# Streaming-encoder layer on one core: second-norm sums from fused additions and squares on ScalarE, stores on three queues, two pairs of the first norm on VectorE, y transposes one tick later

## The chip, the cores and the metric

One core of one Trainium2 chip runs the kernel. The metric is the device time of one execution in microseconds (us); shown is the median of several runs, and beside it one execution that the hardware profiler took.

The engines named below are TensorE (PE in the rows; PEld is its weight load), VectorE (DVE), ScalarE (ACT), GpSimd (POOL) and SyncE (SP). Each works through its instructions in order. Transfers are issued by SP, by POOL or by ACT, each into a queue of its own; only POOL's can add into their destination.

## The reference

The computation is one layer of a hybrid encoder on 1024 tokens of width 1024, all in float32:

```python
mix = hybrid_mixer(x, w_in, b_gate, w_conv, hn_g, w_pool, pool_scale, w_out)
x = layer_norm(ALPHA * x + mix, ln1_g, ln1_b)                            # first norm
x = layer_norm(ALPHA * x + squared_relu_mlp(x, w_ff1, w_ff2), ln2_g, ln2_b)   # second norm

def layer_norm(x, g, b):
    mu = x.mean(-1, keepdims=True)
    var = square(x - mu).mean(-1, keepdims=True)
    return (x - mu) * rsqrt(var + 1e-5) * g + b
```

The mixer projects x to q, k, v, gates and pooling columns, runs a chunkwise mLSTM of four heads (its result per 128 tokens, normalised and gated, is called y below) and a multiscale pooling, and multiplies both by `w_out`. The MLP is `square(relu(x @ w1)) @ w2` with a hidden width of 4096.

## The kernel before, in words

**Number format.** Every f32 matmul is made of three: each operand is split into a high part (a cast on ScalarE, L76) and a low part (a subtraction on VectorE, L77), and `mm3` (L102) issues high x high, high x low and low x high (L103 to L105) into the same PSUM bank.

**Tiles of tokens.** Tokens stand in eight tiles of 128, c = 0 to 7, called tokens 0 to 7 here, in two halves hf = 0 and 1. `z[c, e]` is the accumulator of tile c, column half e (512 wide); `zt[c]` is both halves.

**Order of the work.** The functions at the end of the kernel are called in the order of its text: projections of the first half, of the second half with the mLSTM of the first beside them, and `out_proj(0)` and `out_proj(1)`, the output projection for the two column halves. Side work is put between the matmuls by a clock: `later(lag, fn)` (L111) queues a function, `tick()` (L114) advances the clock by one and runs what is due. A step of a projection (one pair of tiles, 48 matmuls of 512 columns) has two ticks, one in its middle and one at its end. `mlstm(hf)` (L558) splits each tile's mixer into four stages and queues them at four lags; the fourth (after the last `yield` of `mlstm_stages`) transposes y on TensorE (L553) and splits the result into `yTm[c]`, which `out_proj` reads in the second half of the step of the pair that has tile c. Within this, the framework's scheduler settles each engine's final instruction order when the kernel is built, and adds all waits.

**First norm.** `out_proj(e)` goes over pairs cp = 0, 2, 4, 6. For each tile it adds the residual into z (L629) and takes statistics (`bn_stats`, L630). In the pass e = 1 it then aggregates (L633), calls `ln_rsqrt` (L569: a Sqrt on ScalarE, L573, and small VectorE instructions, L574 to L581, with one Newton step) and `ln_apply` (L584) per tile: a ScalarE pass with scale and shift (L588), a multiply by the gain on VectorE (L593 here, L590 for the second norm), and a transfer on POOL that adds the broadcast bias into z (L594). After the pairs cp = 2 and cp = 6 a half is whole, and its z is transposed to the MLP's input (`x1_transpose`, L651, copied to SBUF by ScalarE, L652): half 0 by tasks at lags 3 and 4, half 1 in the job loop at the second job.

**MLP.** Four rounds of two products, each product cut Strassen-fashion into seven jobs of 48 matmuls (i = 1 to 7, `ORDER`, L731). `weights` (L716) loads a 512 KB weight tile by SP (L722) and builds sums of weight blocks by accumulating transfers on POOL (L725); a tile that has been cast for one job grows by another accumulate for the next. In round 0 `x_right` (L754) forms sums of x blocks on VectorE (L746 to L752) and stores them to DRAM by POOL (L762) for the later rounds, where SP loads them (L766). The tiles of the MLP lie in the pool `fq` (21 tiles), which takes the memory of the earlier pool `bigp` (42 tiles), where the gains of the first norm (`gs1`, loaded by POOL at L902) also were.

**Second norm.** `evict2` (L836) adds a product into z (L847). In the last round, jobs 2, 3, 7, 4 are the final ones: statistics are taken of each z (L851). After job 3 the tiles 0 to 3 are aggregated (L857), share one `ln_rsqrt` and go through `ln_apply` and `store` (L866, SP). In job 4, `finish(c)` (L868) does tiles 4 to 7 singly: 4 and 5 by `ln_apply` and `store`; 6 and 7 by (z - mean) x gain (L877) while the root is taken, then x root + bias (L880) and two stores by SP (L881). The gain and bias tiles are `gb2`.

Of the kernel before, what the change touches and what calls it, by code (L numbers as in the profile page):

```python
# [13 lines left out]
ALU = mybir.AluOpType  # L14

P = 128
# [6 lines left out]
def trunk_layer(ctx: ExitStack, tc: tile.TileContext, x, w_in, b_gate, w_conv, hn_g,  # L23
# [534 lines left out]
    def mlstm(hf):  # L558
        for i in range(TT):
            st = mlstm_stages(hf * TT + i)  # L560
            for lag in (max(2 * i - 2, 0), 2 * i + (i == 0), 2 * i + 2, 2 * i + 4):
                later(lag, lambda st=st: next(st, None))
# [6 lines left out]
    def ln_rsqrt(mv, n):  # L569

        v = mv[:, :, 1]
# [28 lines left out]
    def out_proj(e, gs):  # L600
# [3 lines left out]
        for cp in range(0, S // P, 2):  # L604
# [26 lines left out]
            if e == 1:  # L631
                for i in range(2):
                    dve.bn_aggr(mv[:, i, :], st[:, i])  # L633
                r = ln_rsqrt(mv, 2)
                for i in range(2):
                    ln_apply(zt[cp + i], mv, i, r[:, i:i + 1], gs, ln1_b)
# [199 lines left out]
    def evict2(i, ps, r):  # L836
# [4 lines left out]
        for j in range(4):  # L841
            c = t * 4 + j
            zs = z[c, d]
            if r == 0 and i in (1, 6, 5, 4):
# [3 lines left out]
            if final:  # L848
                if c not in ln2:
                    ln2[c] = sml([P, 2, 6], "l2_st", 8)  # L850
                dve.bn_stats(ln2[c][:, d, :], zs)  # L851
            if final and i == 4:
                finish(c)
        if final and i == 3:
            mv = sml([P, 4, 2], "l2_mv4")
            for c in range(4):
                dve.bn_aggr(mv[:, c, :], ln2[c])  # L857
            rr = ln_rsqrt(mv, 4)
            for c in range(4):
                ln_apply(zt[c], mv, c, rr[:, c:c + 1], gb2[:1], ln2_b)  # L860
                store(c)
# [3 lines left out]
    def store(c):  # L865
        sp.dma_start(out[c * P:(c + 1) * P, :], zt[c].rearrange("p e c -> p (e c)"))  # L866

    def finish(c):  # L868
        mv = sml([P, 1, 2], "l2_mv")
        dve.bn_aggr(mv[:, 0, :], ln2[c])  # L870
        if c < 6:
            r = ln_rsqrt(mv, 1)
            ln_apply(zt[c], mv, 0, r, gb2[:1], ln2_b)
            store(c)
            return
        g, b = gb2
        dve.scalar_tensor_tensor(zt[c], zt[c], mv[:, 0, 0:1], g, op0=ALU.subtract, op1=ALU.mult)  # L877
        r = ln_rsqrt(mv, 1)
        for e in C2:
            dve.scalar_tensor_tensor(z[c, e], z[c, e], r, b[:, e, :], op0=ALU.mult, op1=ALU.add)  # L880
            sp.dma_start(out[c * P:(c + 1) * P, e * 512:(e + 1) * 512], z[c, e])  # L881
# [18 lines left out]
    gs1 = [big([P, 512], name="lng") for _ in range(2)]  # L900
    for e in range(2):
# [55 lines left out]
```

## Time and profile before

| | |
|---|---|
| median of 3 runs | 1062.92 us (1061.78 to 1063.1) |
| profiled execution | 1064.35 us |
| its span | 1062.6 us |
| PE busy | 1011.6 us, 95% of the span, 4697 instructions |
| DVE busy | 737.2 us, 69% |
| ACT busy | 446.9 us, 42% |
| POOL busy | 155.6 us, 15% |
| mean granted TensorE clock | 0.983 |
| moved by DMA | 143.29 MB, mean 135 GB/s |

The profiled execution's time holds the span (first to last instruction or transfer of the program, 1062.6 us) and 1.75 us around it. Busy shares are averages over the whole span; the granted clock is a share of TensorE's full speed. Times in rows are microseconds from the span's start unless marked ns.

### The profile page before, as it was taken

The numbers are of one execution on the slowest core, as the hardware profiler recorded it, in microseconds if no ns is written. First come the engines' busy times: TensorE is split into PE (matmuls) and PEld (weight loads), VectorE is DVE, ScalarE is ACT, GpSimd is POOL, SyncE is SP. The second block draws the span as 40 slices with busy tenths as digits, with TensorE's granted clock in tenths as the row PEclk, the third lists the DMA queues.
The fourth block names the chain that finished last, engine by engine and source line by source line (L and its number), as shares of the span: only waits on it lengthen the run. The fifth ranks groups of instructions, "written<-read, shape, count | busy, mean of one in ns | idle before, by whom it ended". The sixth has DMA issues, their size and how long they took to land.

```text
span 1062.6 us, 12549 instructions
## 1 busy us (share of the span) xinstructions
PE 1011.6 (95%) x4697; PEld 826.9 (78%) x4697; DVE 737.2 (69%) x1187; ACT 446.9 (42%) x630; POOL 155.6 (15%) x195
## 2 busy tenths in 40 slices
PE   7999999999989987979999999999999999999991
PEld 5898789778878876858888888888888888888881
DVE  4464775886988445648966478866488875588885
ACT  5334655638322235334433534334524434434441
POOL 2320002312310023200302001302002102001210
PEclk9999999999999998989999999999999999999996
DMA  8411512414421268967807647908737718702728
GB/s 302 135 61 42 158 52 63 137 59 120 159 80 40 60 162 205 272 192 237 154 5 145 196 155 218 159 1 175 223 127 208 138 15 176 257 29 40 143 49 245
DMA packets 64062, 143.29 MB, mean 135 GB/s; under 512 B 4652, under 2 KB 4736, under 8 KB 64000
## 3 DMA queue, kind: packets, MB, share of 16 engines
q1 hardware_dynamic: 41760, 92.09, 26.1%
q0 software_dynamic: 22144, 50.36, 24.8%
q8 instruction: 37, 0.61, 0.2%
q14 instruction: 25, 0.20, 0.1%
q10 hardware_dynamic: 96, 0.03, 0.0%
HBM read 130.90 MB, written 11.57 MB: 134 GB/s over the span
## 4 chain that ended last, share of the span: by engine, by line
PE 82%; DVE 8%; DMA 4%; issue 2%; ACT 1%; POOL 0%; DVEq 0%; SPq 0%; ACTq 0%; POOLq 0%
PE mm L105 17%; PE mm L104 17%; PE mm L103 17%; PE ml L103 5%; PE ml L104 5%; PE ml L105 5%; PE tr L103 5%; PE tr L104 4%; PE tr L105 4%; DMA z<-in_ln_b_dram 2%; DMA w<-in_w_ff_dram 1%; DMA xraw<-in_x_dram 1%; DVE wlo L77 1%; PE tr L651 1%; PE tr L177 1%
## 5 line engine op out<-in xcount | busy, mean ns | idle before, releaser
L77 DVE TENSOR_TENSOR ol<-w,oh 128x1024 fp32r<-128x1024 f32 x112 | 135.6, 1221 | 95.0 <-ACT oh L76 95.0
L103 PE MATMUL mm<-oh,oh 128*128 128x512 f32 x448 | 177.6, 397 | 5.6 <-ACT oh L76 5.6
L76 ACT CAST oh<-w 128x1024 fp32r<-128x1024 f32 x112 | 116.6, 1047 | 152.1 <-PE mm L104 62.6
L104 PE MATMUL mm<-ol,oh 128*128 128x512 f32 x448 | 177.4, 396 | 0.5 <-DVE ol L77 0.5
L105 PE MATMUL mm<-oh,ol 128*128 128x512 f32 x448 | 177.3, 396 | 0.0
L725 POOL DMA_DIRECT2D w<-in_w_ff_dram x64 | 76.9, 1276 | 499.2 <-DVE ol L77 487.4
L103 PEld LDWEIGHTS mm<-oh,oh 128*128 128x128 f32 x448 | 84.8, 189 | 26.0 <-ACT oh L76 6.1
L104 PEld LDWEIGHTS mm<-ol,oh 128*128 128x128 f32 x448 | 84.7, 189 | 20.7 <-DVE ol L77 1.0
L105 PEld LDWEIGHTS mm<-oh,ol 128*128 128x128 f32 x448 | 84.7, 189 | 20.0
L103 PE MATMUL ml<-oh,oh 128*128 128x512 f32 x224 | 88.9, 398 | 0.0
L104 PE MATMUL ml<-ol,oh 128*128 128x512 f32 x224 | 88.8, 396 | 0.0
L105 PE MATMUL ml<-oh,ol 128*128 128x512 f32 x224 | 88.7, 396 | 0.0
L104 PE MATMUL tr<-ol,oh 128*128 128x512 f32 x224 | 88.3, 394 | 0.1
L103 PE MATMUL tr<-oh,oh 128*128 128x512 f32 x224 | 88.3, 394 | 0.0
L105 PE MATMUL tr<-oh,ol 128*128 128x512 f32 x224 | 88.2, 394 | 0.0
L77 DVE TENSOR_TENSOR ol<-xs,oh 128x1024 fp32r<-128x1024 f32 x42 | 51.4, 1224 | 50.7 <-ACT oh L76 50.7
L76 ACT CAST oh<-h 128x1024 fp32r<-128x1024 f32 x40 | 41.7, 1048 | 80.2 <-PE ml L104 24.8
L76 ACT CAST oh<-xs 128x1024 fp32r<-128x1024 f32 x42 | 44.1, 1050 | 66.2 <-PE ml L104 37.3
L77 DVE TENSOR_TENSOR wlo<-raw,whi 128x1024 fp32r<-128x1024 f32 (+1 forms) x44 | 55.2, 1254 | 11.7 <-ACT whi L76 9.0
L76 ACT CAST whi<-raw 128x1024 fp32r<-128x1024 f32 (+1 forms) x44 | 46.0, 1053 | 32.6 <-PE mm L104 13.4
L103 PE MATMUL mm<-xT,whi 128*128 128x512 f32 x144 | 57.3, 398 | 0.1
L104 PE MATMUL mm<-xT,whi 128*128 128x512 f32 x144 | 57.0, 396 | 0.0
(259 smaller groups left out, 1993.0 us busy)
## 6 DMA issues: line engine op xcount, KB each, us to landing
w<-in_w_ff_dram POOLq DMA_DIRECT2D x64, 512.0 KB, 7.5
w<-in_w_ff_dram SPq DMA_DIRECT2D x58, 512.0 KB, 8.2
xs<-xs SPq DMA_DIRECT2D x42, 512.0 KB, 4.7
raw<-in_w_in_dram SPq DMA_DIRECT2D x28, 512.0 KB, 4.3
z<-in_ln_b_dram POOLq DMA_DIRECT2D x14, 512.0 KB, 7.7
xs<-x POOLq DMA_DIRECT2D x12, 512.0 KB, 10.1
raw<-in_w_in_dram SPq DMA_DIRECT2D x8, 520.0 KB, 5.2
raw<-in_w_out_dram SPq DMA_DIRECT2D x8, 512.0 KB, 3.3
```

The source lines that it names most:

```text
L76: act.copy(hi, src)
L77: dve.tensor_tensor(lo, src, hi.bitcast(F32), ALU.subtract)
L103: pe.matmul(ps, lhsT=lh, rhs=rh, start=start, stop=False, skip_group_check=grow)
L104: pe.matmul(ps, lhsT=lh, rhs=rl, start=False, stop=False, skip_group_check=grow)
L105: return pe.matmul(ps, lhsT=ll, rhs=rh, start=False, stop=stop, skip_group_check=grow)
L177: pe.transpose(ps[:, a, b, :], raw[:, b, kc * P:(kc + 1) * P], ident)
L651: pe.transpose(ps[:, j, :], z[hf * TT + j, kb // 4][:, (kb % 4) * P:(kb % 4 + 1) * P], ident)
L725: pool.dma_start(t, w_source(r, ph, q, p), accum_op=ALU.add)
```

## The change

Four places are edited. (1) The fourth lag of `mlstm` goes from 2i + 4 to 2i + 5, capped at 10: for i = 0, 1, 2 of either half the transposes of y come one tick later. (2) In `out_proj(1)`, the pairs cp = 2 and 6 (`late`) no longer use `ln_apply`: VectorE computes (z - mean) x gain in four instructions of 512 columns ahead of `ln_rsqrt`, and z x root + bias in four behind it. For this the bias is loaded as two more tiles (`gs1` has four). (3) In the last round, the final additions into z are one VectorE instruction each that also gives the sum over its 512 columns (`accum_out`); `bn_stats` and `bn_aggr` are gone. `finish(c)` is called for all eight tiles, singly, tiles 0 to 3 behind job 3's evictions: it forms minus the mean, has ScalarE square (z - mean) with the sum as a second output, and takes the root of that. `store` is gone. (4) Stores: tile 5 by POOL, tile 7 by ACT, the others by SP.

```diff
--- before.py
+++ after.py
@@ -558,7 +558,7 @@
     def mlstm(hf):
         for i in range(TT):
             st = mlstm_stages(hf * TT + i)
-            for lag in (max(2 * i - 2, 0), 2 * i + (i == 0), 2 * i + 2, 2 * i + 4):
+            for lag in (max(2 * i - 2, 0), 2 * i + (i == 0), 2 * i + 2, min(2 * i + 5, 10)):
                 later(lag, lambda st=st: next(st, None))
 
 
@@ -566,9 +566,8 @@
     def ln_stats(t, n, tag):
         return sml([P, n, 2, 6], f"{tag}_st{n}"), sml([P, n, 2], f"{tag}_mv{n}")
 
-    def ln_rsqrt(mv, n):
-
-        v = mv[:, :, 1]
+    def ln_rsqrt(v, n):
+
         s, w, t = (sml([P, n], f"l{n}_{i}") for i in "swt")
         act.activation(s, v, AF.Sqrt, bias=epsc)
         dve.tensor_scalar(w, v, EPS, -0.5, op0=ALU.add, op1=ALU.mult)
@@ -631,9 +630,19 @@
             if e == 1:
                 for i in range(2):
                     dve.bn_aggr(mv[:, i, :], st[:, i])
-                r = ln_rsqrt(mv, 2)
+                late = cp % TT == 2
+                if late:
+                    for i, d in ((0, 0), (0, 1), (1, 0), (1, 1)):
+                        zs = z[cp + i, d]
+                        dve.scalar_tensor_tensor(zs, zs, mv[:, i, 0:1], gs[d], op0=ALU.subtract, op1=ALU.mult)
+                r = ln_rsqrt(mv[:, :, 1], 2)
                 for i in range(2):
-                    ln_apply(zt[cp + i], mv, i, r[:, i:i + 1], gs, ln1_b)
+                    if late:
+                        for d in range(2):
+                            zs = z[cp + i, d]
+                            dve.scalar_tensor_tensor(zs, zs, r[:, i:i + 1], gs[2 + d], op0=ALU.mult, op1=ALU.add)
+                    else:
+                        ln_apply(zt[cp + i], mv, i, r[:, i:i + 1], gs[:2], ln1_b)
             if e == 1 and cp % TT == 2:
                 x1_later(cp // TT)
             tick()
@@ -841,44 +850,44 @@
         for j in range(4):
             c = t * 4 + j
             zs = z[c, d]
-            if r == 0 and i in (1, 6, 5, 4):
+            if final:
+                if c not in ln2:
+                    ln2[c] = sml([P, 8], "l2_sum", 8)
+                dve.scalar_tensor_tensor(zs, ps[j], float(sign), zs, op0=ALU.mult, op1=ALU.add,
+                                         accum_out=ln2[c][:, d:d + 1])
+                if i in (3, 4):
+                    finish(c)
+            elif r == 0 and i in (1, 6, 5, 4):
                 dve.scalar_tensor_tensor(zs, zs, ALPHA, ps[j], op0=ALU.mult, op1=op)
             else:
                 dve.tensor_tensor(zs, zs, ps[j], op)
-            if final:
-                if c not in ln2:
-                    ln2[c] = sml([P, 2, 6], "l2_st", 8)
-                dve.bn_stats(ln2[c][:, d, :], zs)
-            if final and i == 4:
-                finish(c)
-        if final and i == 3:
-            mv = sml([P, 4, 2], "l2_mv4")
-            for c in range(4):
-                dve.bn_aggr(mv[:, c, :], ln2[c])
-            rr = ln_rsqrt(mv, 4)
-            for c in range(4):
-                ln_apply(zt[c], mv, c, rr[:, c:c + 1], gb2[:1], ln2_b)
-                store(c)
 
     ln2, gb2 = {}, []
 
-    def store(c):
-        sp.dma_start(out[c * P:(c + 1) * P, :], zt[c].rearrange("p e c -> p (e c)"))
-
     def finish(c):
-        mv = sml([P, 1, 2], "l2_mv")
-        dve.bn_aggr(mv[:, 0, :], ln2[c])
+
+        q = ln2[c]
+        neg, ss, s, w, u, shift = (q[:, k:k + 1] for k in range(2, 8))
+        zf, (g, b) = zt[c], gb2
+        dve.tensor_scalar(neg, q[:, 0:1], q[:, 1:2], -1.0 / 1024, op0=ALU.add, op1=ALU.mult)
+        act.activation(quad("sq"), zf, AF.Square, bias=neg, accum_out=ss)
+        if c >= 6:
+            dve.scalar_tensor_tensor(zf, zf, neg, g, op0=ALU.add, op1=ALU.mult)
+        act.activation(s, ss, AF.Sqrt, bias=epsc, scale=1.0 / 1024)
+        dve.tensor_scalar(w, ss, -0.5 / 1024, -0.5 * EPS, op0=ALU.mult, op1=ALU.add)
+        dve.reciprocal(s, s)
+        dve.scalar_tensor_tensor(u, s, s, w, op0=ALU.mult, op1=ALU.mult)
+        dve.scalar_tensor_tensor(s, u, 1.5, s, op0=ALU.add, op1=ALU.mult)
         if c < 6:
-            r = ln_rsqrt(mv, 1)
-            ln_apply(zt[c], mv, 0, r, gb2[:1], ln2_b)
-            store(c)
+            dve.tensor_tensor(shift, neg, s, ALU.mult)
+            act.activation(zf, zf, AF.Identity, scale=s, bias=shift)
+            dve.tensor_tensor(zf, zf, g, ALU.mult)
+            pool.dma_start(zf, b, accum_op=ALU.add)
+            (pool if c == 5 else sp).dma_start(out[c * P:(c + 1) * P, :], zf.rearrange("p e c -> p (e c)"))
             return
-        g, b = gb2
-        dve.scalar_tensor_tensor(zt[c], zt[c], mv[:, 0, 0:1], g, op0=ALU.subtract, op1=ALU.mult)
-        r = ln_rsqrt(mv, 1)
         for e in C2:
-            dve.scalar_tensor_tensor(z[c, e], z[c, e], r, b[:, e, :], op0=ALU.mult, op1=ALU.add)
-            sp.dma_start(out[c * P:(c + 1) * P, e * 512:(e + 1) * 512], z[c, e])
+            dve.scalar_tensor_tensor(z[c, e], z[c, e], s, b[:, e, :], op0=ALU.mult, op1=ALU.add)
+            (act if c == 7 else sp).dma_start(out[c * P:(c + 1) * P, e * 512:(e + 1) * 512], z[c, e])
 
     proj_o(0)
     small_parameters()
@@ -897,9 +906,10 @@
     proj_qk(1, 0)
     later(1, lambda: mlstm(1))
     proj_p(1)
-    gs1 = [big([P, 512], name="lng") for _ in range(2)]
-    for e in range(2):
-        after(pool.dma_start(gs1[e], ln1_g[0:1, e * 512:(e + 1) * 512].to_broadcast([P, 512])), anchor[0])
+    gs1 = [big([P, 512], name="lngb") for _ in range(4)]
+    for e in range(4):
+        src = (ln1_g, ln1_b)[e // 2][0:1, e % 2 * 512:(e % 2 + 1) * 512]
+        after(pool.dma_start(gs1[e], src.to_broadcast([P, 512])), anchor[0])
     out_proj(0, gs1)
     out_proj(1, gs1)
```

## Rows read from the trace of the kernel before

**Rows 1.** TensorE's waits, whole span: line <- waited for: us in total, times, longest
```profile
PE tr L651 <- DMA z<-in_ln_b_dram: 8.8, 4, 4.0
PE mm L103 <- ACT oh L76: 5.6, 1, 5.6
PE tr L553 <- DVE y L549: 4.9, 3, 2.8
```
**Rows 2.** Timeline of TensorE, L651: start, us, engine, operation [idle before <- releaser]
```profile
380.08 0.74 PE L651 MATMUL tr<-ident,z 128*128 128x128 f32 x5 [2.52 <-DMA z<-in_ln_b_dram]
...
411.92 0.45 PE L651 MATMUL tr<-ident,z 128*128 128x128 f32 x1 [4.01 <-DMA z<-in_ln_b_dram]
414.38 1.30 PE L651 MATMUL tr<-ident,z 128*128 128x128 f32 x5 [2.01 <-DMA z<-in_ln_b_dram]
```
**Rows 3.** Stretches: us, then each engine's busy us, PEclk, DMA share, GB/s
```profile
375.00:385.00 10.00, 7.18 (x32) 5.71 (x31) 5.00 (x14) 3.27 (x6) 1.12 (x2) 0.83 0.56 134
408.00:424.00 16.00, 10.07 (x50) 8.45 (x51) 8.96 (x9) 9.42 (x15) 5.72 (x6) 0.79 1.01 203
424.00:440.00 16.00, 16.00 (x70) 13.01 (x70) 14.94 (x15) 5.40 (x6) 5.54 (x9) 1.00 1.02 341
```
**Rows 4.** Chain of waits, around the transposes of z: start, us, engine and line
```profile
373.43 6.52 DMA z<-in_ln_b_dram
...
404.45 9.79 DMA z<-in_ln_b_dram
...
415.68 0.85 PE ml L103 x2
...
418.80 0.87 PE tr L651 x8
419.67 0.23 PE ml L105
```
**Rows 5.** Timeline of all engines, the tail from 1040 us
```profile
1040.84 0.39 PE L105 MATMUL ml<-oh,ol 128*128 128x512 f32 x1
...
1044.21 0.69 DVE L851 BATCH_NORM_STATS2 l_st<-z 128x6 f32<-128x512 f32 x1
...
1046.56 0.86 POOL L594 DMA_DIRECT2D z<-in_ln_b_dram  x1 [1.78 <-issue]
...
1049.36 1.41 DVE L880 SCALAR_TENSOR_TENSOR z<-z,l_s,lngb 128x512 f32<-128x512 f32 x2
...
1055.84 0.33 SPq L866 DMA_DIRECT2D out_dram<-z  x1
1056.59 0.87 SPq L881 DMA_DIRECT2D out_dram<-z  x2
```
**Rows 6.** Timeline of VectorE, first norm of cp = 6 and job 1's operands
```profile
398.75 0.17 DVE L574 TENSOR_SCALAR l_w<-l_mv 128x2 f32<-128x2 f32 x1
399.08 0.17 DVE L575 RECIPROCAL l_s<-l_s 128x2 f32<-128x2 f32 x1 [0.16 <-ACT l_s L573]
...
401.40 2.50 DVE L593 TENSOR_TENSOR z<-z,lng 128x512 f32<-128x512 f32 x4 [1.30 <-ACT z L588]
...
408.63 1.23 DVE L77 TENSOR_TENSOR ol<-x,oh 128x1024 fp32r<-128x1024 f32 x1 [0.21 <-ACT oh L76]
```
**Rows 7.** Timeline of POOL, mixer's work for token 6 and later stores of x sums
```profile
298.68 1.19 POOL L507 TENSOR_TENSOR vs<-v,g_ep 128x516 f32<-128x516 f32 x1 [6.22 <-DVE ps L352]
...
450.07 0.57 POOL L762 DMA_DIRECT2D xs<-x  x1 [9.63 <-DVE x L752]
```
**Rows 8.** Waits of SP's queue, 395 to 430 us
```profile
SPq L722 <- DVE z L593: 14.1, 1, 14.1
```
**Rows 9.** Groups of ScalarE, whole span: busy us, mean ns, idle before
```profile
L588 ACT ACTIVATE z<-z,l_sh,l_s 128x1024 f32<-128x1024 f32 x14 | 16.6, 1235 | 9.2 <-DVE l_sh L587 9.2
...
L573 ACT ACTIVATE l_s<-l_mv,epsc 128x2 f32<-128x2 f32 (+2 forms) x9 | 2.7, 295 | 37.3 <-DVE l_mv L633 27.6 <-DVE l_mv L870 7.6 <-DVE l_mv L857 2.0
...
L573 ACT ACT_TABLE_LOAD x1 | 1.3, 1283 | 0.0
```

## Prediction, made before the changed kernel was run

> **What bounds the kernel now.** I read the table of TensorE's waits first, because TensorE is busy 95% of the span and a wait counts only where it stands still. There are few such places [rows 1]: the transposes of the first norm's output (L651) wait 8.8 us for the transfer that adds the bias into z, the transposes of the mixer's y (L553) wait 4.9 us for VectorE, and one wait of 5.6 us is for a cast of operands. Then the timeline of TensorE at L651: 4.01 and 2.01 us belong to the pair cp = 6, so 2.8 of the 8.8 to cp = 2 [rows 2]. The clock view shows what a stall costs beyond itself: the mean granted clock is 0.83 and 0.79 in the two stretches with these waits and 1.00 in the next [rows 3], and in the chain of waits matmuls follow each other in 0.43 us behind the second stall and in 0.23 a little later [rows 4]: the lower and the higher of the clock's two levels (1.2 and 2.4 GHz). Last, the tail: the last matmul starts at 1040.84 [rows 5], 21.8 us before the span ends at 1062.6.
>
> **The sum is made against the profiled execution, 1064.35 us, which stands 1.43 us over the median of 1062.92.** A difference under 0.2% (2.1 us) could not be told from none.
>
> **First norm, last pairs.** For cp = 2 and 6 the change takes away two ScalarE passes, four multiplies by the gain and two bias transfers per pair, and puts four VectorE instructions ahead of the reciprocal square root and four behind it. At cp = 6 the aggregates are out by 398.75 [rows 6]. The new instructions have the form of L880, two in 1.41 us [rows 5], 0.70 apiece. Four make 2.8; ScalarE's root runs beside them; one small instruction before it and four behind (a pitch of 0.2 from the reciprocal at 399.08) make 1.0; four more make 2.8. z is whole at 405.3, which is 1.4 us after the multiplies' old end (401.40 + 2.50 [rows 6]), but no transfer follows. TensorE comes for it at 411.92 - 4.01 = 407.91 [rows 2]: both waits go, with 2.6 us to spare. For cp = 2 the bias transfer was under way at 373.43 [rows 4], some 0.5 us after the multiplies; 1.4 us on from there z is whole at 374.3, and TensorE stood waiting from 380.08 - 2.52 = 377.56. Together 8.8 us.
>
> L880 reads two f32 tensors out of SBUF and costs 0.70 us for 512 columns; the plain multiply of the same width costs 2.50 / 4 = 0.63 [rows 5, 6]. The Trainium skill (Vector Engine (DVE) Microarchitecture Reference, "Points that are easy to get wrong") says that a scalar-tensor-tensor with two such sources runs at half throughput. These rows don't agree; by it, as an estimate from twice 0.63, z would be whole at 409.8, 1.9 us of waiting would be left, and the sum would be 2 us smaller.
>
> With the stalls goes the lower clock behind them. From 415.68 to 418.80 eight matmuls took 3.12 us, at 0.23 they take 1.84 (1.3 less); ahead of them five transposes took 1.30 where eight take 0.87 later (0.75 less) [rows 2, 4]: 2.0 us. Behind cp = 2 I take half, 1.0 us (bounds 0 and 2.0).
>
> What is late next: job 1's operands. VectorE subtracts their x low half at 408.63 [rows 6], done at 409.86, and TensorE, with eight transposes (0.87 us) and one matmul done from 407.91, would want it at 409.0. I charge 0.5 us (0, since the cast ahead may come earlier when ScalarE loses two passes, to 2.0, since VectorE's own work grows by 3.1: eight of 0.70 for four of 0.63). So cp = 2 gives 2.8 + 1.0 = **3.8 us** and cp = 6 gives 6.0 + 2.0 - 0.5 = **7.5 us**. Two more loads, of the bias, are put on POOL's queue ahead of the mixer's work for token 6; POOL stood idle 6.22 us ahead of that [rows 7], so they cost 0, and without that cover 0.6 us each (by the issue at 450.07).
>
> **The later stall.** The 5.6 us wait for a cast, at 470, ends a chain that TensorE drives only in part: SP's weight load waits 14.1 us for z's multiplies by the gain, whose memory it takes [rows 8]; then come cast, accumulate on POOL and cast again, with the DMA engines full (share 1.01 and 1.02 from 408 to 440 [rows 3]). If it doesn't move, the stall grows by what cp = 6 gains, 7.5 us. But the gain is now last read by the first four new instructions, at 401.6 and no longer 403.9, so that load may leave 2.3 us earlier, and the two bias transfers beside it (the second 9.79 us [rows 4]) are gone. If all of it moves along, the loss is 0. No row decides between 0 and -7.5; I take the middle, **-3.5 us**.
>
> **y transposes.** For six of the eight tokens they move one tick on, half a projection step, 24 matmuls of 0.23 = 5.5 us; tokens 3 and 7 stay (the cap of 10 equals 2 x 3 + 4). The three waits hold 4.9 us, the longest 2.8 [rows 1]: each fits into 5.5. The y tile lives that much longer, and the casts and subtractions of y come later on ScalarE and VectorE; the output projection takes y only in the second half of a pair, at the soonest one tick behind the latest new place. Behind them on TensorE stand the matmuls of the next half step, which don't read y; a backlog of VectorE that showed here may show at one that reads something else of its work. I take 4.9 - 0.5 = **4.4 us** (bounds 0 and 4.9).
>
> **The tail.** The end is a chain of transfers: token 5's bias transfer is issued on POOL at 1046.56; its store stands on SP until 1055.84, 9.3 us later; and token 7's two stores, whose data VectorE had ready at 1050.8, stand behind it until 1056.59, the last issue ending at 1057.5, 5.1 us before the span does [rows 5]. After the change token 7's stores go by ScalarE's queue, behind nothing. Per token VectorE loses a statistics pass (0.69 us [rows 5]) and an aggregate and gains a small sum and an accumulator read; no row shows the read, and I price the three small ones alike, at 0.17 [rows 6] (read: 0 to 0.17). Ahead of token 5's last multiply stand three tokens by 0.5 us, of which I take 1.3 as they overlap: its transfer leaves at 1045.2. It takes 6.5 to 9.8 us to land [rows 4]; I take 8, since the first four tokens, now finished singly, send their stores earlier: 1053.2. POOL then issues the store in 0.57 us (as at 450.07 [rows 7]), and 5.1 us on it has landed: 1058.9, 3.7 us earlier. Token 7 is in time: from 1041.2, evict 0.7, sum 0.2, square 1.24 as L588 and its read 0.2, root 0.3 [rows 9], four small of 0.2, two of 0.70, 4.8 us in all, with VectorE's and ScalarE's queues nearer 1049, landing by 1055. I take **3.0 us** (0 to 5). The squares of the first four tokens I cost at 0; if a cast of the last operands stood behind them, four of 1.24 would be 5 us at the worst.
>
> **Sum:** 3.8 + 7.5 - 3.5 + 4.4 + 3.0 = 15.2 us; 1064.35 - 15.2 = 1049.1, by the median 1047.7.
>
> **The rivals.**
> 1. *The weight chain doesn't move* (0.20): the stall grows by all of 7.5. For it: the full DMA engines; against: fewer and earlier transfers. 11.2 us gained, **1051.7**.
> 2. *Token 5 on POOL lands late* (0.11): at 9.8 us, like the slower bias transfer on the same queue [rows 4], it ends at 1063.6, 1.0 us after the old end; against: that one ran among weight loads. 11.2 gained, **1051.7**.
> 3. *The change doesn't do what it says* (0.08): VectorE's order puts operand subtractions (1.23 us each [rows 6]) between the new instructions, and z comes no sooner than TensorE; two per pair and job 1's behind them bring back 5 us as waits for VectorE, **1052.7**.
> 4. *Square and Sqrt need different tables* (0.03). The table for Sqrt was loaded once, in 1.28 us, and ScalarE's L588 runs between roots without another [rows 9]. If Square needs its own, the last four tokens have eight loads, 10 us in a row on ScalarE; about half has the stores to hide behind, and the end comes 5 us late instead of 3 early: 7.2 gained, **1055.7**. The Trainium skill (ScalarE: Activation LUTs, "Table sets: the hidden batching unit") says cheap functions are in every set, but its list doesn't name Square; the 2.66 us that "What ACT_TABLE_LOAD costs" there gives for a switch would make it some 11 us worse.
> 5. *Slower: the weight chain slips by a job* (0.09). Place: POOL's queue, where the weights' accumulates stood behind stores of x sums that waited 9.63 us for VectorE [rows 7]. If such a store comes between once more, the chain stays (7.5), slips a job of 48 matmuls (11.0), and the lower clock is paid once more (2.0): 20.5 against gains of 18.7, **1064.7**. It decides from a stall of 24.3 us (5.6 + 18.7); a lesser slip ends at no change.
>
> **How the numbers follow.** The forecast has 0.49. Below, 7.5 us kept whole and 5 in the tail make 20.7 us, so the low end is 1042.5; above, rivals 1 to 4 are inside at 1057. Left out are rival 5 and the edges, under 2 in 10. Faster 0.91; same 0.03 and slower 0.06, both out of rival 5.
>
> **What would show it.** Right: no wait for a bias transfer at L651; waits at L553 under 1 us; the span's end 18.8 us behind the last matmul's start; the wait for a cast, near 454, between 5.6 and 13 us. Wrong: L651 waiting for VectorE, table loads between squares and roots, the store of token 5 landing past the old distance, or a stall over 24 us.

## The result and the profile after

The changed kernel takes 1049.61 us (median of 4 runs, 1049.24 to 1051.44) where the kernel before takes 1063.01 (4 runs beside them, 1061.78 to 1063.46): ratio 0.9879, 95% interval 0.9862 to 0.9896, so 13.4 us faster by the medians (the ratio is that of the mean times). Forecast were 1047.7 us and a range of 1042.5 to 1057.0. The profiled execution took 1049.71 us with a span of 1048.0; against the execution on which the sum was made (1064.35, span 1062.6) that is 14.6 us less, and the sum said 15.2.

That the total came out is in part luck: two terms of the sum are wrong by over 7 us each, in opposite directions. First the table of TensorE's waits of the changed kernel, whole span (line <- waited for: us in total, times, longest), to be read beside [rows 1]:

```profile
PE tr L553 <- DVE y L549: 3.2, 1, 3.2
PE ml L524 <- ACT o L518: 2.8, 2, 2.0
PE ml L103 <- ACT oh L76: 2.7, 1, 2.7
PE tr L660 <- ACT x L661: 2.3, 2, 1.7
PE mm L103 <- ACT oh L76: 2.2, 1, 2.2
```

The transposes of z (now L660) wait for no transfer any more: 8.8 us are gone. But a new wait of 2.7 us for a cast has come up; the wait for y has gone from 4.9 us to 3.2 only; and the later stall, forecast to grow from 5.6, has shrunk to 2.2. The same three in the timeline of TensorE of the changed kernel (start, us, operation, [idle before <- releaser]):

```profile
310.53 0.66 PE L553 MATMUL tr<-ident,y 128*128 128x128 f32 x4 [3.24 <-DVE y L549]
...
405.55 0.73 PE L103 MATMUL ml<-oh,oh 128*128 128x512 f32 x2 [2.68 <-ACT oh L76]
...
460.53 0.50 PE L103 MATMUL mm<-oh,oh 128*128 128x512 f32 x1 [2.20 <-ACT oh L76]
```

To size the terms, cut both traces at the same instructions: the first addition into z of cp = 2 in the second pass, that of cp = 6, TensorE's stop before the later stall (the start of its row less the idle time), the last matmul's start, and the span's end. The windows of the two middle stretches hold the same number of TensorE's rows in both kernels (columns as in [rows 3]). Before:

```profile
364.94:395.89 30.95, 28.13 (x129) 22.63 (x128) 15.00 (x37) 11.43 (x16) 5.68 (x8) 0.94 0.60 140
395.89:464.46 68.57, 62.43 (x275) 50.02 (x273) 39.09 (x47) 27.34 (x36) 17.05 (x20) 0.95 0.93 251
```

After:

```profile
363.79:390.19 26.40, 26.32 (x129) 21.30 (x128) 17.55 (x39) 9.05 (x14) 4.02 (x6) 1.00 0.47 113
390.19:458.33 68.14, 62.66 (x275) 49.53 (x273) 42.95 (x50) 26.98 (x38) 15.40 (x18) 0.97 0.90 257
```

| stretch | before, us | after, us | gained | forecast |
|---|---|---|---|---|
| start to cp = 2 (y transposes) | 364.94 | 363.79 | 1.15 | 4.4 |
| cp = 2 to cp = 6 | 30.95 | 26.40 | 4.55 | 3.8 |
| cp = 6 to the later stall | 68.57 | 68.14 | 0.43 | 7.5 |
| later stall to the last matmul (1040.84; 1030.80) | 576.38 | 572.47 | 3.91 | -3.5 |
| last matmul to the end (1062.6; 1048.0) | 21.76 | 17.20 | 4.56 | 3.0 |
| sum | 1062.6 | 1048.0 | 14.6 | 15.2 |

**Where cp = 6's gain went.** z itself comes as forecast. VectorE's timeline of the changed kernel at cp = 6:

```profile
392.94 2.73 DVE L637 SCALAR_TENSOR_TENSOR z<-z,l_mv,lngb 128x512 f32<-128x512 f32 x4
...
396.43 2.74 DVE L643 SCALAR_TENSOR_TENSOR z<-z,l_s,lngb 128x512 f32<-128x512 f32 x4
```

Four in 2.73 us, 0.68 apiece, and z is whole at 399.17, 2.7 us before TensorE transposes it at 401.84. What is late is the second weight tile of job 1, as the chain of waits of the changed kernel shows (start, us, engine and line):

```profile
397.10 2.08 DVE z L643 x3
...
399.24 0.37 SPq L731
...
440.51 0.53 POOL xs L771
...
442.17 0.73 POOL w L734
442.90 15.03 DMA w<-in_w_ff_dram
...
459.54 0.95 ACT oh L76
```

SP's load leaves at 399.24, right behind the last of the eight new instructions. ScalarE's timeline shows the rest: the cast of that tile stands 2.50 us for its data, the cast of x behind it ends at 405.50, and TensorE starts at 405.55:

```profile
403.03 1.04 ACT L76 CAST oh<-w 128x1024 fp32r<-128x1024 f32 x1 [2.50 <-DMA w<-in_w_ff_dram]
...
404.45 1.05 ACT L76 CAST oh<-x 128x1024 fp32r<-128x1024 f32 x1
```

And the table of the waits of SP's queue, 385 to 430 us, says how long that load had stood there:

```profile
SPq L731 <- DVE z L643: 24.0, 1, 24.0
```

By the addresses of the built program this weight tile lies where the tile of the bias's second half was, which the last new instruction reads. In the kernel before, no gain tile lay under a weight tile of job 1, only under job 2's, where the wait of [rows 8] belongs. Among the other kernels that have the new first norm the two go together: where SP's load waits 24.0 us for the last new instruction (e6_y5, e7_vec7, e8_x4sp, e10_sp, e12_swap), TensorE waits 2.6 to 2.8 us for job 1's cast; where it doesn't (e2_late, e4_early, e5_nolag, e9_both, e11_t5), that wait isn't there.

### The profile page after: what moved, and what is told of

It reads as the page before. It is cut to its first block, busy times and chain, and to the rows that moved or that the text cites. A ratio compares the mean times of both kernels' runs of the same rounds, so it can differ in the third digit from the quotient of the medians.

```text
span 1048.0 us, 12564 instructions
## 1 busy us (share of the span) xinstructions
PE 1008.4 (96%) x4697; PEld 824.5 (79%) x4697; DVE 733.1 (70%) x1202; ACT 451.1 (43%) x645; POOL 155.8 (15%) x194
## 4 chain that ended last, share of the span: by engine, by line
PE 80%; DVE 8%; DMA 5%; issue 4%; ACT 2%; POOL 1%; SPq 0%; POOLq 0%; ACTq 0%; DVEq 0%
PE mm L103 17%; PE mm L105 17%; PE mm L104 17%; PE ml L103 5%; PE ml L105 5%; PE ml L104 5%; PE tr L103 4%; PE tr L104 4%; PE tr L105 4%; DMA w<-in_w_ff_dram 3%; DMA xraw<-in_x_dram 1%; DVE wlo L77 1%; DVE ol L77 1%; DMA xres<-in_x_dram 1%; PE tr L177 1%
## 5 line engine op out<-in xcount | busy, mean ns | idle before, releaser
L76 ACT CAST whi<-raw 128x1024 fp32r<-128x1024 f32 (+1 forms) x44 | 46.1, 1053 | 33.6 <-PE mm L104 13.4
```

Of the source, the lines that this page charges most:

```text
L76: act.copy(hi, src)
```

## The experiments

All in one table, each with the ratio to the kernel before that ran beside it (medians of before: 1063.4 us for the first four, 1062.65 for the next four, 1062.42 for the last four):

| run | median, us (range) | ratio, 95% interval |
|---|---|---|
| e1_lag | 1060.04 (1057.95 to 1062.12) | 0.9968 (0.9956 to 0.998) |
| e2_late | 1052.83 (1052.66 to 1053.32) | 0.9902 (0.9889 to 0.9916) |
| e3_tail | 1057.16 (1056.74 to 1058.98) | 0.9948 (0.9934 to 0.9961) |
| e4_early | 1049.99 (1048.89 to 1050.63) | 0.9874 (0.986 to 0.9887) |
| e5_nolag | 1048.16 (1047.16 to 1049.22) | 0.9859 (0.9841 to 0.9877) |
| e6_y5 | 1051.66 (1051.22 to 1054.51) | 0.9898 (0.988 to 0.9916) |
| e7_vec7 | 1049.64 (1048.31 to 1050.72) | 0.9872 (0.9854 to 0.9891) |
| e8_x4sp | 1045.31 (1044.22 to 1047.33) | 0.9832 (0.9813 to 0.9852) |
| e9_both | 1042.71 (1041.68 to 1044.63) | 0.9815 (0.9793 to 0.9838) |
| e10_sp | 1049.91 (1047.9 to 1052.16) | 0.9875 (0.9854 to 0.9897) |
| e11_t5 | 1039.1 (1038.54 to 1039.53) | 0.9774 (0.9754 to 0.9795) |
| e12_swap | 1044.38 (1042.17 to 1045.9) | 0.9824 (0.9803 to 0.9844) |

### The parts, one at a time

Three kernels have one part of the change each, on the kernel before: the lag of y, the pairs cp = 2 and 6 with their bias tiles, and the tail (sums, squares, stores). The lag alone is one line:

```diff
-            for lag in (max(2 * i - 2, 0), 2 * i + (i == 0), 2 * i + 2, 2 * i + 4):
+            for lag in (max(2 * i - 2, 0), 2 * i + (i == 0), 2 * i + 2, min(2 * i + 5, 10)):
```

> Only the later tick of the y transposes, on the kernel before. Theory (from the trace of the changed kernel): token 5's transposes keep their place in TensorE's order, so its wait of 2.8 us stays or grows to about 3.2 and only the waits of tokens 2 and 4 (1.65 and 0.47) go: 1.2 us faster, and TensorE's waits at L553 sum to 2.8 to 3.3. Rival (the prediction's step): all three waits go, 4.4 us faster.

The lag alone takes the waits for y down to 0.5 us, as the rival had it, and the addition of cp = 2 comes at 361.79, 3.15 us earlier than before; the 3.4 us of the medians lie between theory and rival. At the last matmul of the profiled execution (1039.81) 1.0 us is left, and the rest of its 2.5 lies behind the last matmul, where the lag changes nothing. What is lost is lost in part at the transposes of z, and the later stall is longer, as TensorE's timeline of this run shows beside the 5.6 us of [rows 1]:

```profile
469.10 0.80 PE L103 MATMUL mm<-oh,oh 128*128 128x512 f32 x1 [6.26 <-ACT oh L76]
```

> Only the last pairs of the first norm on VectorE (with the four tiles of gain and bias), on the kernel before. Theory: cp = 2 gives 4.6 us; at cp = 6 the 6 us of waits for the bias transfer come back almost whole as a wait for job 1's weights, whose load waits for the bias tiles' memory, and the later stall shrinks from 5.6 to 2.2: 8.9 us faster in all. Rival (the prediction's sum): 3.8 + 7.5 - 3.5 = 7.8 us faster, with no wait at job 1 over 0.5 us and a later stall of 5.6 to 13 us.

The pairs alone give most of the change, 10.6 us, more than either the theory or the rival had. The stretch from cp = 2 to cp = 6 is as short as in the whole change (26.37 us), and there is no wait of 2.7 us for job 1's cast; the later stall is 2.69 us here too.

> Only the second norm: sums out of the last additions, squares on ScalarE, stores on three queues, on the kernel before. Theory: the distance from the last matmul's start to the span's end falls from 21.8 to 17.2 us, 4.6 us faster, nothing else moves. Rival (the prediction): 3.0 us faster. If the three parts don't add up to the whole change (13.4), they act on each other.

The tail alone gives 6.2 us, more than the 4.6 of the theory. Between the two profiled spans it is 7.5: 5.4 in the distance from the last matmul to the end (16.3 us), and the last matmul comes 2.1 us earlier, mostly by a later stall of 4.46 us. Why that stall is shorter in this run was not followed up. A single execution's stall doesn't say much, though: in e10_sp, whose built program is that of the changed kernel up to the last stores, it took 3.80 us where the changed kernel's profile has 2.20.

The parts alone add up to 3.4 + 10.6 + 6.2 = 20.2 us, the whole gives 13.4: something that each gains alone is given back in company.

The changed kernel without the lag closes the other side:

> The changed kernel with its y part undone: the fourth lag is 2i + 4 again, all else as changed. What it lacks is the y part in the company of the others. Forecast's price of that part (4.4 us): 1054.0 us. Its price alone on the kernel before (1063.4 - 1060.04 = 3.4 us): 1053.0. Rival, that the first norm, the weight chain and the job loop behind it take back nearly all of what the y part gains by 365 us (last matmul of that run only 1.0 us earlier): 1049.6 to 1050.6, with waits of TensorE for y (L549) of 5 to 6 us in sum, and the last matmul's start within 1 us of 1030.8.

It is no slower but rather faster, 1048.16, under all three of the times expected. Without the lag cp = 2 comes later (366.03, so the lag is worth at most 2.2 us there; the waits for x at the start differ by 1.7, 6.7 against 5.0), but from cp = 6 to the later stall the changed kernel needs 68.14 us and this one 63.71:

```profile
392.41:456.12 63.71, 61.42 (x275) 48.17 (x273) 42.94 (x50) 26.67 (x37) 15.35 (x18) 1.00 0.98 283
```

Without the lag the build gives the gain and bias tiles other addresses (the lag changes which tiles are alive when memory is given out): no bias or gain tile lies under job 1's weights, and the wait for their cast is gone. So in company the lag gives at most 2.2 us and takes 4.4; the two medians differ by less than their intervals can tell, but a gain of 4.4 us is excluded. Of the 6.8 us by which the parts alone exceed the whole, these 4.4 are the share whose cause is known.

### The memory under job 1's weights

```diff
+    gs1 = [big([P, 512], name="lngb") for _ in range(4)]
+    for e in range(4):
+        ...
     later(1, lambda: mlstm(1))
     proj_p(1)
-    gs1 = [big([P, 512], name="lngb") for _ in range(4)]
-    for e in range(4):
-        ...
```

> The changed kernel with the four gain and bias tiles of the first norm allocated and loaded one projection earlier (ahead of the last pooling projection), so that they take other memory: SP's loads for job 1 no longer wait for VectorE, the first load for job 2 does. Theory: job 1's waits for casts (3.2 us) go, TensorE's first norm transposes run on, and since job 2's load still waits for the last read of the bias, the later stall grows by what is gained: within 2 us of the changed kernel. Rival: the chain follows TensorE and 3 to 4 us are gained, 1046.

With the four tiles taken and loaded one projection earlier, the wait for job 1's cast goes, and the stretch behind cp = 6 is 1.6 us shorter (66.50 us, from 392.50). A wait of 3.06 us for ScalarE's copies of the transposed z comes up in its place, and the mixer's tiles move too: L524 and L496 wait 4.7 and 3.0 us (2.8 and 1.3 in the changed kernel), and cp = 2 comes 2.4 us later. The sum is nought: the theory's time, but not by its way, since the later stall did not grow (2.1 us).

```diff
     gs1 = [big([P, 512], name="lngb") for _ in range(4)]
+    gs1 = gs1[2:] + gs1[:2]
...
-                pool.dma_start(d, t)
+                (sp if i == 4 else pool).dma_start(d, t)
```

> The changed kernel with the stores of job 4's x sums on SP's queue (1045.3 us alone), and the four tiles of gain and bias in exchanged places, so that job 1's second weight tile comes to lie where the gains were, read last by the first four new instructions of cp = 6, and no longer where the biases were, read last by the second four. No engine's order differs from that run. Theory (this memory is where the gain at cp = 6 went): SP's load leaves some 3 us earlier (near 398 and not 401), the wait for job 1's cast (2.6 + 0.5 us) goes or falls under 1 us, with it the lower clock from 405 to 424 us (0.91): 1041.0 to 1043.0. Rival (the next of the loads, now behind the biases, is late in its place): a wait of 2 to 3 us at the next operand, 1044.4 to 1046.

This edit did not do what it says. The wait of SP's queue is unchanged, because the build gave the exchanged tiles exchanged addresses, so that the bias's second half lies under the same weight tile as before:

```profile
SPq L731 <- DVE z L643: 24.0, 1, 24.0
```

Its time, 1044.38, is that of e8_x4sp below within the ranges; of the theory it says nothing.

### The wait for y

```diff
         for h in range(4):
-            pe.transpose(pt[:, h, :], y[:, h, :], ident)
+            tr = pe.transpose(pt[:, h, :], y[:, h, :], ident)
+            if c == 5:
+                after(tr, anchor[0])
...
-                    mm3(ps, lh, ll, wh[:, kb % 2, :], wl[:, kb % 2, :], n == 0, n == KB - 1)
+                    anchor[0] = mm3(ps, lh, ll, wh[:, kb % 2, :], wl[:, kb % 2, :], n == 0, n == KB - 1)
```

and the lag of token 5 set to 8.

> The changed kernel with token 5's transposes of y held half a projection step further back on TensorE, behind the last matmul issued before them (in the changed kernel they kept their place, and TensorE waited 3.2 us there). Theory: that wait goes, cp = 2 comes 1.5 to 3 us earlier, but the mixer's other waits (L496, L516, L524) grow by a part of it, and behind cp = 6 at most half is left: 1048.5 to 1049.6. Rival (the forecast's own reasoning, a wait removed is time gained): 3.2 us, 1046.4. Worse than 1050.5 would mean that token 5's late casts of y hold up the output projection.

Both theory and rival miss: nothing is gained, 2 us more by the medians, which the intervals don't tell from no change. The wait for y goes, and at the same place TensorE waits for VectorE all the same, now for the additions into z that read the projection's PSUM bank:

```profile
311.42 0.50 PE L103 MATMUL mm<-whi,yph 128*128 128x512 f32 x1 [2.61 <-DVE z L630]
```

So the wait at 310 is a backlog of VectorE, not a matter of where the transposes stand.

Part of that backlog has a curious cause. VectorE's timeline of the changed kernel has two instructions of 128x4 elements that take seven times their usual 0.17 us:

```profile
303.65 1.25 DVE L464 TENSOR_SCALAR r_y<-r_w 128x4 int32<-128x4 int32 x1
304.94 1.23 DVE L465 TENSOR_SCALAR r_y<-r_y 128x4 int32<-128x4 int32 x1
```

and GpSimd's timeline has two tensor operations that end 0.03 and 0.04 us before they do (303.65 + 1.25 = 304.90 against 304.87; 306.17 against 306.13):

```profile
303.58 1.29 POOL L489 TENSOR_TENSOR ng<-ng,mask 128x512 f32<-128x512 f32 x1 [4.33 <-DMA ng<-bounce]
304.83 1.30 POOL L499 TENSOR_TENSOR si<-si,qk 128x512 f32<-128x512 f32 x1
```

```diff
-        pool.tensor_tensor(ng, ng, mask.unsqueeze(1).to_broadcast([P, 4, P]), ALU.add)
+        eng = dve if c == 7 else pool
+        eng.tensor_tensor(ng, ng, mask.unsqueeze(1).to_broadcast([P, 4, P]), ALU.add)
...
-            pool.tensor_tensor(si, si, q, ALU.mult)
+            eng.tensor_tensor(si, si, q, ALU.mult)
```

> The changed kernel with token 7's two tensor operations of 1.3 us each (ng, si) taken off GpSimd and put on VectorE. In the changed kernel two VectorE instructions of 128x4 elements took 1.25 and 1.23 us where the same lines take 0.17 elsewhere, and each ended as one of GpSimd's two ended. Theory (a VectorE instruction that starts while GpSimd's tensor operation runs is held until that ends): none of VectorE's instructions of 128x4 between 300 and 312 us takes over 0.3 us. Rival (they are slow by themselves there, or held by something else): one or two still take 1.1 to 1.3. In time: VectorE saves 2.1 us of holding and takes on two of 0.69, so y of token 5 is at best 0.7 us earlier and the whole the same within 1 us, 1048.6 to 1050.6.

The theory holds. The same lines in VectorE's timeline of this run:

```profile
305.11 0.17 DVE L464 TENSOR_SCALAR r_y<-r_w 128x4 int32<-128x4 int32 x1
305.32 0.17 DVE L465 TENSOR_SCALAR r_y<-r_y 128x4 int32<-128x4 int32 x1
```

TensorE's wait for y falls from 3.2 to 1.1 us and cp = 2 comes 0.9 us earlier (362.93); a new wait of 1.5 us for a cast on ScalarE at 321.67 and the stalls behind leave the whole where it was.

The lag alone (e1_lag) showed the same without being meant to. There token 5's transposes stand within four matmuls of their old place too, but GpSimd's second operation was over at 304.09, before VectorE came to these lines, and TensorE waited 0.5 us:

```profile
302.81 1.28 POOL L499 TENSOR_TENSOR si<-si,qk 128x512 f32<-128x512 f32 x1
304.55 0.17 DVE L464 TENSOR_SCALAR r_y<-r_w 128x4 int32<-128x4 int32 x1
```

So of the waits that the lag took away alone, token 5's part (2.8 to 0.5 us) goes with a collision that this run happened to miss, and not with where the transposes stand. Why GpSimd's operations came earlier there was not tried.

### The later stall

On GpSimd's queue two accumulates of weights stand behind two stores of x sums, which wait for VectorE's last x sum (in the chain above: store at 440.51, accumulate at 442.17, 15.03 us of transfer, cast, TensorE at 460.53). The edit is the second half of the diff of e12_swap: those two stores go by SP.

> The changed kernel with the two stores of the last x sums of round 0 (job 4 of 7) issued by SP and no longer by GpSimd. On GpSimd's queue they wait 7.7 us for VectorE's last x sum (440.5 us), and the two accumulating transfers of the weights behind them, of which one takes 15 us, end in the stall of 2.2 us at 460. Theory (that place in the queue is what sets the later stall): the accumulates leave near 432 to 434, the wait for a cast at 460 goes (2.2 + 0.8 us), with it the lower clock behind it (0.90 from 458 to 475, 1 to 1.7 us): 1045.2 to 1046.6. Rival (the accumulates are held by the casts of the job before or by full DMA engines, and the place in the queue only hides it): stall within 0.7 us of before, 1049.0 to 1050.2.

The theory holds, 4.3 us better than the changed kernel. GpSimd's timeline of this run has the two accumulates 6.6 and 3.9 us earlier (in the changed kernel they stood as a pair of 2.50 us from 442.17, the second so at 443.4), waiting only for earlier transfers:

```profile
433.99 0.58 POOL L771 DMA_DIRECT2D xs<-x  x1 [2.18 <-DVE x L759]
435.57 1.20 POOL L734 DMA_DIRECT2D w<-in_w_ff_dram  x1 [1.00 <-DMA w<-in_w_ff_dram]
439.53 1.23 POOL L734 DMA_DIRECT2D w<-in_w_ff_dram  x1 [2.76 <-DMA w<-in_w_ff_dram]
```

and TensorE stands nowhere between 440 and 475 us, at a granted clock of 1.00:

```profile
440.00:458.00 18.00, 18.00 (x79) 14.50 (x78) 10.36 (x10) 10.70 (x15) 0.76 (x1) 1.00 1.07 324
458.00:475.00 17.00, 17.00 (x75) 13.65 (x74) 17.00 (x20) 6.37 (x7) 0.00 (x0) 1.00 0.45 144
```

In the changed kernel the second of these windows had 14.04 us of TensorE at 0.90. Together with the undone lag:

> The changed kernel with two edits that were tried singly: the y part undone (1048.2 us alone) and the two stores of job 4's x sums on SP's queue (4.3 us better alone). Theory (the two act at different places and add): 1048.2 - 4.3 = 1043.9 us, 1042.5 to 1044.7, with no wait for a cast over 1 us between 400 and 480 us. Rival (both give back the same delay of the weight chain, so the second adds little): 1045 to 1046.5, no better than the stores alone.

The theory holds, and the two add: 1042.71, with no wait for a cast over 0.6 us left behind cp = 6.

### The tail

```diff
-            (pool if c == 5 else sp).dma_start(out[c * P:(c + 1) * P, :], zf.rearrange("p e c -> p (e c)"))
+            sp.dma_start(out[c * P:(c + 1) * P, :], zf.rearrange("p e c -> p (e c)"))
...
-            (act if c == 7 else sp).dma_start(out[c * P:(c + 1) * P, e * 512:(e + 1) * 512], z[c, e])
+            sp.dma_start(out[c * P:(c + 1) * P, e * 512:(e + 1) * 512], z[c, e])
```

> The changed kernel with all stores of the output on SP's queue again (tokens 5 and 7 too); nothing else differs. Theory: token 5's store waits on SP for the bias transfer until about 10 us behind the last matmul, token 7's two stand behind it and leave some 1.5 us later than token 5's store leaves in the changed kernel: end 1.2 to 1.9 us later, 1050.8 to 1051.5. Rival (token 5's bias transfer and its own store alone set the end): 1049.0 to 1050.2.

The rival holds: the time is the same, and the distance from the last matmul (1032.46) to the end (1048.6) is 16.1 us; in the changed kernel and the eight other runs with its tail it lies between 16.3 and 17.2. Token 7's stores do leave later, as SP's timeline shows, yet nothing is lost:

```profile
1042.24 0.33 SPq L886 DMA_DIRECT2D out_dram<-z  x1
1042.99 1.05 SPq L890 DMA_DIRECT2D out_dram<-z  x2
```

From the last issue's end to the span's end it is 1048.6 - 1044.04 = 4.6 us by SP; in the changed kernel, where token 5's store by GpSimd is the last, 1048.0 - 1041.41 = 6.6. So of the tail's gain the three queues give nothing that shows.

```diff
-        if c >= 6:
+        if c >= 5:
             dve.scalar_tensor_tensor(zf, zf, neg, g, op0=ALU.add, op1=ALU.mult)
...
-        if c < 6:
+        if c < 5:
...
-            (act if c == 7 else sp).dma_start(out[c * P:(c + 1) * P, e * 512:(e + 1) * 512], z[c, e])
+            (act if c == 7 else pool if c == 5 else sp).dma_start(out[c * P:(c + 1) * P, e * 512:(e + 1) * 512], z[c, e])
```

> As e9_both, and token 5 finished like tokens 6 and 7: gain and bias on VectorE, two stores on GpSimd's queue, no bias transfer at its end. In the changed kernel the chain of the end is token 5's bias transfer (6.0 us) and its store; token 7's last store leaves about 1 us earlier than token 5's. Theory: the transfer goes from the end, but VectorE has 1.28 + 1.41 - 1.22 = 1.5 us more ahead of token 7, which becomes the end: the distance from the last matmul's start to the span's end goes from 17.2 to 16.2 to 17.7, so the same as e9_both within 1 us. Rival (the transfer is the whole of the end's length): 15 us or less, 2 us better than e9_both.

The rival holds, and more: 3.6 us better than e9_both. The distance is 1036.8 - 1023.92 = 12.9 us where e9_both has 17.2. Token 7's stores leave no earlier, counted from the last matmul (8.5 us; 8.1 in the changed kernel), but the span ends 3.4 us behind their last issue, as ScalarE's timeline and the span show:

```profile
1032.41 1.02 ACTq L890 DMA_DIRECT2D out_dram<-z  x2
```

My theory charged VectorE's 1.5 us, of which 0.4 shows at those stores, and left out that they land sooner: the median from issue to landing of those on ScalarE's queue is 2.2 us here and 4.0 in e9_both. That they do so because no bias transfer runs beside them is likely, but was not tried by itself. At 1039.1 us this is the fastest version: the change, without its lag, with job 4's stores of x sums on SP and token 5 finished on VectorE.

## Why the prediction was right, step by step

The direction and the size came out; of the five terms two were near (cp = 2 and the tail), one gave a quarter of what was forecast (y), and two were wrong by 7.1 us too much and 7.4 too little. That these cancel is luck, not mechanism. Of the signs of being right that the prediction named, only the first came, no wait for a bias transfer at the transposes; the wait for y was 3.2 us and not under 1, the end stood 17.2 us behind the last matmul's start and not 18.8, and the wait for the cast was 2.2 us and not 5.6 to 13.

**cp = 2: 3.8 forecast, 4.55 measured.** The mechanism was right: the wait is gone, and the granted clock of the stretch goes from 0.94 to 1.00. TensorE's idle time falls from 30.95 - 28.13 = 2.8 us to 0.1, as forecast. The clock was the mis-sized part: its busy time falls by 1.8 us, where I took half of a bound of 2.0.

**cp = 6: 7.5 forecast, 0.43 measured.** The step that failed is "What is late next: job 1's operands". I looked at the x operand only and charged 0.5 us. Job 1's second weight tile was late, because a tile that the change adds lies under it, and the lower clock came with the stall again: 0.91 from 405 to 424 us. The edit's own text shows two more tiles; I costed their loads on GpSimd's queue, which were indeed free, and not the memory that they hold and free late. Where the collision is absent (e5_nolag), the stretch gains 4.9 us, still not 7.5: TensorE's idle time there is 63.71 - 61.42 = 2.3 us against 6.1 before, since it now waits 1.7 us for ScalarE's copies of the transposed z, which stand among the casts.

**The later stall: -3.5 forecast, +3.91 measured.** The failed step is "If all of it moves along, the loss is 0": it lets the chain of weights move at most as far as TensorE does, and the result lies outside both bounds, 0 and -7.5. The store of an x sum left at 450.07 before [rows 7] and leaves at 440.51 now, 9.6 us earlier, while TensorE's stop comes 6.1 us earlier (464.46 to 458.33), so the stall shrinks by 3.4. The start of the chain was not wrong: the changed kernel's chain above runs back to SP's load at 399.24. What was left out is, first, the place of two accumulates behind the stores of x sums on GpSimd's queue, which holds the stall in the changed kernel, as e8_x4sp shows; I had that very row [rows 7] and used it only for rival 5. Second, VectorE's order: the subtraction of a weight's low half, which releases an accumulate on GpSimd, stood behind the instructions that gather h, and the build of the changed kernel puts it ahead of them, as VectorE's timelines show. Before:

```profile
427.86 1.23 DVE L77 TENSOR_TENSOR ol<-xt,oh 128x1024 fp32r<-128x1024 f32 x1 [0.58 <-ACT oh L76]
...
432.66 1.22 DVE L77 TENSOR_TENSOR ol<-w,oh 128x1024 fp32r<-128x1024 f32 x1
```

After:

```profile
421.07 1.23 DVE L77 TENSOR_TENSOR ol<-xt,oh 128x1024 fp32r<-128x1024 f32 x1 [0.59 <-ACT oh L76]
422.21 1.22 DVE L77 TENSOR_TENSOR ol<-w,oh 128x1024 fp32r<-128x1024 f32 x1
```

The accumulate leaves at 423.73 (434.18 before), the cast that waits for it starts at 436.76 (446.33), and behind that cast's subtraction VectorE forms the x sum for whose store the queue stands. The old order is also that of e1_lag and e3_tail, with stalls of 6.3 and 4.5 us; the new one that of e2_late, e4_early, e5_nolag, e6_y5 and e10_sp, with 2.1 to 4.2. The order was not changed by itself, and of the 3.4 us some 1.6 may be the difference between executions (2.20 and 3.80 above).

**y transposes: 4.4 forecast, 1.15 measured.** The failed step is "each fits into 5.5": the longest wait did not move back with the tick. Token 5's transposes kept their place among the matmuls, and its wait stayed (2.8 before, 3.24 now); the waits of the two other tokens went. The place was not what held it, though: forcing the transposes back (e6_y5) only moved the wait, and at the same place it fell to 1.1 and 0.5 us where VectorE was not held by GpSimd (e7_vec7, e1_lag). The words "a backlog of VectorE that showed here may show at one that reads something else of its work" were the right warning, priced at 0.5 us. Alone the lag gave 3.15 us at cp = 2; in company it also changes the memory under job 1's weights and is worth nothing at the end (e5_nolag).

**The tail: 3.0 forecast, 4.56 measured.** The chain was right: token 5's bias transfer, then its store. The mis-sized term is the transfer's landing. In the changed kernel's timeline it leaves 4.05 us behind the last matmul (5.72 before, so 1.7 us sooner; 1.3 forecast) and its store is issued when it has landed, 6.0 us later, where I took 8 and before had 9.3:

```profile
1030.80 0.40 PE L105 MATMUL ml<-oh,ol 128*128 128x512 f32 x1
...
1034.85 0.86 POOL L885 DMA_DIRECT2D z<-lngb  x1 [3.06 <-issue]
...
1038.94 1.71 ACTq L890 DMA_DIRECT2D out_dram<-z  x2
...
1040.85 0.56 POOL L886 DMA_DIRECT2D out_dram<-z  x1 [5.14 <-DMA z<-lngb]
```

From that store's end to the span's end it takes 6.6 us, not 5.1. "Token 7 is in time" was right. Part of the 4.56 is the execution that the sum was made against: its distance of 21.76 us is the longest of the three runs with the old tail (20.3 in e1_lag, 20.5 in e2_late), so that with 16.3 to 17.2 for the new one the tail is worth 3.1 to 5.4 us.

**The rivals.** Rival 1 is refuted: the weight chain moved more than TensorE. Rival 2 as well: it had token 5's store land 9.8 us behind its issue, and the span ends 6.6 us behind it. Rival 3 did not happen at cp = 6: z was whole before TensorE came. Rival 4 is refuted by ScalarE's groups of the changed kernel (busy us, mean ns | idle before), whose squares and roots have no table load between them:

```profile
L873 ACT ACTIVATE sq<-z,l_sum 128x1024 f32<-128x1024 f32 x8 | 9.2, 1147 | 10.4 <-DVE l_sum L872 10.4
...
L876 ACT ACTIVATE l_sum<-l_sum,epsc 128x1 f32<-128x1 f32 x8 | 2.3, 287 | 0.1
...
L873 ACT ACTIVATION_READ_ACCUMULATOR sq<-z,l_sum 128x1 f32 x8 | 1.5, 186 | 0.0
```

The Trainium skill (ScalarE: Activation LUTs, "Table sets: the hidden batching unit") has cheap functions in every set, and the trace agrees for Square beside Sqrt, which its list doesn't name. Rival 5 named the right queue and the wrong direction.

The new VectorE instructions, two f32 sources out of SBUF and 0.68 us for 512 columns, settle the other rule weighed there: the Trainium skill (Vector Engine (DVE) Microarchitecture Reference, "Points that are easy to get wrong") has half throughput for them, and the trace does not agree.

## What to carry to other kernels

When a change adds a tile or lets one live longer, ask what will be given its memory next and which instruction frees it: here that took back the largest term, and a shift of the mixer by half a step switched it on. Read a stall's own chain of waits back to the queue in which it stands before pricing how it moves; moving two stores to another queue was worth a third of the whole change. And a transfer at the very end costs its own landing, and the stores beside it landed later: 1.5 us of VectorE in its place were cheaper by 3.6 us. Last, a total that comes out says little about its terms: only the cut at the same instructions showed that two of them were wrong.

## What the runs showed of the hardware

A VectorE instruction of 128x4 elements that normally takes 0.17 us took 1.25 and 1.23 us while GpSimd ran a tensor operation, and ended 0.03 to 0.04 us after it; with that operation taken off GpSimd it took 0.17 (e7_vec7). The Trainium skill (SBUF — State Buffer, "Who interferes with whom") says that GpSimd and VectorE, in a mode in which VectorE uses two ports, contend for a pair that they share: whoever issues first has it for the whole instruction, and the other is fully blocked. The trace agrees as far as it goes; the mode of these instructions it doesn't show. I had not looked for it at this place, though the profile of before has such rows too.

The second output of an instruction has a row of its own: 0.19 us on ScalarE behind a square (above) and 0.08 us on VectorE behind an addition into z. I had taken 0.2 and up to 0.17.
